# A 512-byte read on each of the sixteen DMA engines, queued ahead of the first load of an RMS norm

## Chip, cores and metric

One core of a Trainium2 chip. The metric is the device time of one execution in microseconds, as the median of several runs. "Span" is the part of an execution that the profile covers; it is about 1.8 us shorter than the measured time. A packet is one piece of a transfer, moved by one of the core's sixteen DMA engines.

## The reference

```python
def setup_inputs():
    batch, seq, dim = 16, 1024, 512
    # x: float32 randn (16, 1024, 512); gamma: ones(512); eps: 1e-5

def reference(x, gamma, eps):
    rms = np.sqrt(np.mean(x ** 2, axis=-1, keepdims=True) + eps)
    x_norm = x / rms * gamma
    return np.maximum(x_norm, 0).astype(np.float32)
```

The input is 33.5 MB and the output as much. The work per element is small, so the transfers decide.

## The kernel before

The rows are cut into eight chunks of 4 MB (16 rows on each of 128 partitions, 32 KB a partition). Six slots in SBUF hold chunks. SyncE, which does no arithmetic here, issues all loads and stores of chunks; the first chunk is loaded in two halves. ScalarE squares and sums, VectorE scales and clamps in place, and the slot is stored from where it lies. GpSimd only turns "load landed" into a count for ScalarE.

```python
    loads = [(0, 0, G), (0, G, K - G)] + [(i, 0, K) for i in range(1, nchunks)]
    ...
    def load(m):
        i, a, r = loads[m]
        nc.sync.dma_start(out=slot_ap(i)[:, a:a + r, :],
                          in_=xv[i][:, a:a + r, :]).then_inc(sem_ld[m], 16)
    ...
    with tc.tile_critical():
        for m, (i, a, r) in enumerate(loads):
            if i < nslots:
                load(m)                      # seven loads, issued at once
        nxt = nslots
        for i in range(nchunks):
            nc.sync.wait_ge(done, per * (i + 1))
            store(i)
            if i >= 1 and nxt < nchunks:
                nc.sync.wait_ge(sem_st[nxt - nslots], 16)
                ...                          # load of chunk nxt into the freed slot
        for m, (i, a, r) in enumerate(loads):
            nc.gpsimd.wait_ge(sem_ld[m], 16)
            nc.gpsimd.sem_inc(ready, r // G)

        nc.vector.memset(gseed, 0.0).then_inc(sem_z, 1)
        nc.vector.memset(eps_sb, eps).then_inc(sem_e, 1)

        nc.scalar.wait_ge(sem_z, 1)
        nc.scalar.dma_start(out=gseed[0:P:32, :], in_=...gamma...).then_inc(sem_g, 16)
        ...                                  # the loops of ScalarE and VectorE
```

## Time and profile before

| | before |
|---|---|
| time, median of six runs | 162.82 us (162.61 to 162.89) |
| span of the profiled run | 161.2 us |
| DMA queue of SyncE, share of sixteen engines | 97.4% |
| VectorE, ScalarE busy | 78%, 54% |
| first load issued, first packet | 0.94 us, 1.95 us |

The prediction was made from three of these runs, whose median was 162.71 us. The transfers are busy from 1.95 us to the end, so a change can only pay off by starting the stream earlier, by losing less of it, or by ending it better. The lines of the profile for this are in the prediction. One line more, for comparison with the kernel after: the instructions of SyncE in order of time, at the start (columns: start, length in us, engine, line, operation, tiles, count).

```profile
0.94 3.59 SPq L74 DMA_DIRECT2D slots<-in_x_dram  x7
```

Seven loads are issued in one go from 0.94 us on, each some 0.4 to 0.7 us of SyncE's time.

### The profile page before, as it was taken

Reading aid. Unit: us, or ns where it says so; the run is one execution under the profiler, and the core shown is the slowest. Engines: PE = TensorE matmul, PEld = TensorE weight load, DVE = VectorE, ACT = ScalarE, POOL = GpSimd, SP = SyncE. Lnnn points to the kernel's source line nnn. Section 1 sums busy time; section 2 is a strip of 40 time slices with the busy share of each in tenths; the row PEclk is TensorE's granted clock in tenths of the full one; section 3 lists DMA queues with packets and bytes.
Section 4 is the critical chain, followed back from the end, with each engine's and each line's share of the span. In section 5 each row is a group of like instructions: output and inputs, shape, how many; then the busy total and the mean of one; then the engine's idle time right before and its main releaser. Section 6 shows DMA issues by size and latency. Waiting matters only on the chain. (4 is left out here: it accounts for less than half of the span.)

```text
span 161.2 us, 1006 instructions
## 1 busy us (share of the span) xinstructions
DVE 126.0 (78%) x164; ACT 86.3 (54%) x273; POOL 0.2 (0%) x4
## 2 busy tenths in 40 slices
DVE  1103989898989898999999999999999999993000
ACT  3088929889988988988900298503994000000000
POOL 0000000000000000000000000000000000000000
DMA  5999999999999999999999999999999999999993
GB/s 155 433 439 431 496 390 415 496 390 399 512 390 390 512 399 390 390 399 512 390 399 504 399 399 496 407 399 488 407 407 488 407 407 480 415 407 464 431 390 138
DMA packets 2456, 67.12 MB, mean 416 GB/s; under 512 B 276, under 2 KB 276, under 8 KB 280
## 3 DMA queue, kind: packets, MB, share of 16 engines
q1 hardware_dynamic: 2448, 67.11, 97.4%
q10 hardware_dynamic: 8, 0.01, 0.0%
HBM read 33.56 MB, written 33.55 MB: 416 GB/s over the span
## 5 line engine op out<-in xcount | busy, mean ns | idle before, releaser
L115 ACT ACTIVATE junk<-slots 128x512 f32 x128 | 74.5, 582 | 30.8 <-ACTq L111 30.5
L139 DVE SCALAR_TENSOR_TENSOR slots<-slots,rstd,gamma_sb 128x512 f32 x128 | 86.2, 747 | 4.8 <-DVEq L136 4.8
L146 DVE TENSOR_SCALAR slots<-slots x16 | 36.7, 2294 | 2.4 <-DVEq L145 0.2
L115 ACT ACTIVATION_READ_ACCUMULATOR junk<-slots x128 | 23.9, 187 | 0.0
L133 DVE RECIPROCAL rstd<-rms x16 | 3.2, 197 | 6.4 <-DVEq L129 6.4
L122 ACT ACTIVATE rms<-ss,eps_sb x16 | 4.8, 301 | 3.0 <-ACTq L121 3.0
L126 DVE LOAD_MASK_SELECT gamma_sb<-gseed x1 | 0.0, 14 | 5.8 <-DMA gseed<-in_gamma_dram 5.8
L107 ACT ACT_TABLE_LOAD x1 | 1.3, 1283 | 2.8 <-issue 2.8
L100 DVE MEMSET gseed<- 128x512 f32 x1 | 0.5, 485 | 1.1 <-SPq L81 1.1
L126 DVE STREAM_SHUFFLE gamma_sb<-gseed 128x512 f32<-128x512 f32 x1 | 0.7, 716 | 0.0
L168 POOL MEMSET const-bfloat16-1.0<- 128x1 bf16 x1 | 0.1, 102 | 0.0
L168 POOL MEMSET const-uint8-127<- 128x1 uint8 x1 | 0.1, 102 | 0.0
L168 POOL MEMSET const-float32-1.0<- 128x1 f32 x1 | 0.1, 99 | 0.0
L168 POOL MEMSET const-float32-0.0<- 128x1 f32 x1 | 0.1, 98 | 0.2 <-issue 0.2
L101 DVE MEMSET eps_sb<- 128x1 f32 x1 | 0.1, 59 | 0.0
## 6 DMA issues: line engine op xcount, KB each, us to landing
out_dram<-slots SPq DMA_DIRECT2D x8, 4096.0 KB, 31.4
slots<-in_x_dram SPq DMA_DIRECT2D x7, 4096.0 KB, 30.4
slots<-in_x_dram SPq DMA_DIRECT2D x2, 2048.0 KB, 9.7
gseed<-in_gamma_dram ACTq DMA_DIRECT2D x1, 8.0 KB
```

The lines of the kernel that those rows point to most:

```text
L100: nc.vector.memset(gseed, 0.0).then_inc(sem_z, 1)
L101: nc.vector.memset(eps_sb, eps).then_inc(sem_e, 1)
L107: nc.scalar.preload_act_table(ACTF.Sqrt)
L115: a = nc.scalar.activation(out=junk[:, j, :], in_=slots[:, bass.ds(base + j * d, d)], func=ACTF.Square, accum_out=ss[:, bass.ds(col + j, 1)])
L122: nc.scalar.activation(out=rms[:, bass.ds(col, G)], in_=ss[:, bass.ds(col, G)], func=ACTF.Sqrt, bias=eps_sb, scale=inv_d).then_inc(sq, 1)
L126: nc.vector.stream_shuffle(gamma_sb, gseed, [0] * 32)
L133: nc.vector.reciprocal(out=rstd[:, bass.ds(col, G)], in_=rms[:, bass.ds(col, G)]).then_inc(sv, 1)
L139: r = nc.vector.scalar_tensor_tensor(out=row, in0=row, scalar=rstd[:, bass.ds(col + j, 1)], in1=gamma_sb, op0=ALU.mult, op1=ALU.mult)
L146: nc.vector.tensor_scalar_max(out=blk, in0=blk, scalar1=0.0).then_inc(done, 1)
L168: nc = _bacc.Bacc("TRN2", target_bir_lowering=False, num_devices=1)
```

## The change

The intent: the first packets of the first load take about twice as long as later ones. A small read on every DMA engine (below: the **touch**), put ahead of that load, might take this start-up loss on itself. Its data is not used.

```diff
+    scratch = singles.tile([16, 128], F32, name="scratch")
...
+    sem_t = tc.alloc_semaphore("touch")
...
     with tc.tile_critical():
+        nc.sync.dma_start(out=scratch, in_=xv[0][0:P:P // 16, 0, 0:128]
+                          ).then_inc(sem_t, 16)
         for m, (i, a, r) in enumerate(loads):
             if i < nslots:
                 load(m)
...
+        nc.gpsimd.wait_ge(sem_t, 16)
         for m, (i, a, r) in enumerate(loads):
             nc.gpsimd.wait_ge(sem_ld[m], 16)
```

## The prediction

> **What bounds the kernel now.** I read the page of the kernel before from its second part down: the engine table, the 40 slices, the DMA queues, then the chain that ended last, the DMA issues, and finally the stretches of time around the start and the end.
>
> ```profile
> span 161.2 us, 1006 instructions
> DVE 126.0 (78%) x164; ACT 86.3 (54%) x273; POOL 0.2 (0%) x4
> DMA  5999999999999999999999999999999999999993
> GB/s 155 433 439 431 496 390 415 496 390 399 512 390 390 512 399 390 390 399 512 390 399 504 399 399 496 407 399 488 407 407 488 407 407 480 415 407 464 431 390 138
> q1 hardware_dynamic: 2448, 67.11, 97.4%
> ```
>
> The reader should see three things. No compute engine is full (VectorE 78%, ScalarE 54%). The DMA row is 9 in every slice but the first and the last, and one queue, SyncE's, keeps the sixteen engines busy for 97.4% of the span. And the two slices that are not full are the ones that the change could touch: the first (5 tenths, 155 GB/s) is the start of the stream. The chain that ended last is of no help here, because it holds only the last VectorE instruction and does not follow the stores.
>
> Is the transfer queue ever short of work? The issues answer it.
>
> ```profile
> core 0 of [0], span 161.2 us
> engine line waited for: us in total, times, longest us
> SPq L78 <- DVE slots L146: 105.4, 6, 26.6
> SPq L74 <- DMA out_dram<-slots: 32.9, 2, 24.1
> SPq L151 <- DMA out_dram<-slots: 12.5, 2, 9.6
> ```
>
> SyncE waits 105.4 us for VectorE before it can issue stores, which looks like a bound by VectorE. It is not: the first store is issued at 31.1 us, but by the trace's completion events the loads already queued land until 62.3 us, so the store stands in the queue behind them. The tightest place is the end: the last store is issued at 146.5 us and the store ahead of it lands at 150.4 us. So VectorE has about 3.9 us in hand where it is tightest, and the stream of transfers alone sets the end. That stream is one line: it starts at some time, then moves 67.1 MB at its rate, and the end is start plus volume over rate. Only the start can move here.
>
> The stretches of time show the start (columns: stretch, its length, VectorE busy, ScalarE busy, GpSimd busy, TensorE clock, DMA share, GB/s; a packet counts where it begins, so short stretches can pass 1.00):
>
> ```profile
> 0.00:0.94 0.94, 0.00 (x0) 0.00 (x0) 0.20 (x4) 1.00 0.00 0
> 0.94:1.90 0.96, 0.49 (x2) 0.00 (x0) 0.00 (x0) 1.00 0.00 0
> 1.90:2.50 0.60, 0.00 (x0) 0.00 (x0) 0.00 (x0) 1.00 1.65 328
> 2.50:3.10 0.60, 0.00 (x0) 0.34 (x1) 0.00 (x0) 1.00 0.29 109
> 3.10:3.70 0.60, 0.00 (x0) 0.60 (x1) 0.00 (x0) 1.00 1.09 437
> 3.70:10.00 6.30, 0.72 (x2) 1.56 (x5) 0.00 (x0) 1.00 0.99 420
> 158.50:161.20 2.70, 0.00 (x0) 0.00 (x0) 0.00 (x0) 1.00 0.00 0
> ```
>
> The first load is issued at 0.94 us and the first packet starts at 1.95 us. In the stretch from 1.90 to 2.50 us, twelve packets of 16 KB begin (328 GB/s times 0.60 us is 197 KB), and their recorded time fills 1.65 of it, far more than such packets normally take; then almost nothing begins until 3.1 us. The packet records say the same one by one: the twelve first packets took 1.18 to 1.49 us (mean 1.32 us), while the later 16 KB packets of the first two loads take 0.611 us. So these engines lose about 0.7 us each on their first packet. The other four engines begin theirs late, at 2.61 to 3.02 us; one of those took 0.92 us, the other three about 0.61. All sixteen first packets end at 3.17 to 3.63 us. If a packet needs 0.611 us of moving, data really moved from 2.56 to 3.02 us at the earliest, whatever start is recorded. This start-up delay is what a small read ahead could be meant to absorb.
>
> **What the Trainium skill says.** "DMA: Bandwidth & Descriptors", section "Where 436 GB/s comes from", gives a ceiling of about 435 GB/s for sixteen engines. This trace agrees: a 32 KB packet takes 1.213 us, so sixteen engines move 16 x 32768 B / 1.213 us = 432 GB/s, and no faster middle is to be had. The same page, section "Latency and other measured facts", gives about 0.6 us to the first byte for a transfer issued from SyncE or ScalarE. The trace shows more: 1.01 us from issue to the first packet's start, and at least 1.6 us to the first data moving. The section "Queues, rings and completion order" says that on each engine descriptors are consumed in ring order and a later one may finish its write earlier. So the sixteen touches go ahead of the load's own descriptors, and the load is not held for their writes. The section "Why a DMA increments its semaphore by 16 and not by 1" says how many engines a copy uses: the largest number up to 16 that divides both outer dimensions. Both are 16 here, so each engine gets one 512-byte read, as intended. The trace of the kernel before cannot show these last two; the order and the number of packets after can. No section I found says that a first read warms anything.
>
> **The change, part by part.**
>
> It removes nothing. It adds one SyncE issue ahead of the first load, sixteen 512-byte packets with sixteen semaphore writes, one wait on GpSimd, and an unused tile of 512 bytes on 16 partitions.
>
> 1. The issue. The first two loads are issued at 0.94 and 1.375 us, 0.435 us apart, so the first load should now be issued near 1.375 us and its first packet can start at 1.95 + 0.435 = 2.38 us. All later issues move back alike, but they queue behind a full stream and cost nothing.
>
> 2. The packets. In the trace, a 2048-byte packet of the gamma load takes 84 ns and a 4-byte semaphore write 9 ns. In a straight line between them, 512 bytes take an estimated 28 ns; with its semaphore write, 37 ns on each engine. All of it lies on the stream: +0.04 us.
>
> 3. The start-up delay. It now falls on the touch, which is issued when the load was (0.94 us), so it ends when it ended before, at 2.56 to 3.02 us. The load's descriptors, there from 2.38 us on, wait behind it and then run at 0.611 us. That hides the issue delay of step 1 but wins nothing, because the delay runs from the same time: the touch can start no earlier than the load did. For the twelve early engines the net is step 2's +0.04 us. The four engines that started last (2.61, 2.83, 2.84, 3.02 us) may start their load 0.435 us later again if their lateness comes from the handing out of descriptors and not from the first access. Then the net there is up to +0.43 us.
>
> 4. GpSimd's wait for the touch ends by about 3.5 us, well before the first load lands at 8.4 us, where its next wait ends. Free. If ScalarE starts 0.2 us later than its 8.78 us, VectorE's path moves back by the same, against 3.9 us in hand. Free too.
>
> Sum: between +0.04 and +0.43 us; I take the middle, +0.2 us, so 162.71 + 0.2 = 162.9 us.
>
> **The rivals.**
>
> The warm-up wins. If what makes first packets slow is the load's large form (its 128 descriptors) and a small touch gets past it quicker, first packets would run at 0.611 us from 2.38 us on and end at about 3.0 us in place of a mean of 3.4 us: -0.4 us, or 162.3 us. For it: the mean excess of 0.7 us exceeds the 0.435 us that the touch costs. Against it: all sixteen first packets end within 0.46 us, even those that began a microsecond later, which looks like a delay from the start of traffic and not like a cost of each packet.
>
> The warm-up fails. If the excess belongs to the load's own first write into its tile, or to its own source pages on the remaining partitions, it is paid after the touch again. Then the whole issue delay stays: +0.435 + 0.04 = +0.47 us, or 163.2 us; should the touch's own delay be added in full, some +0.7 us more, 163.9 us. For it: the touch writes to another tile than the load. Against it: of the sixteen second packets most take 0.611 us at once, though they too are first accesses to their rows.
>
> VectorE takes over the end. It would need a shift of over 3.9 us between the first landing and the stores; nothing in a touch of under a microsecond makes that. In that case the time would be above 166 us.
>
> The phases change. One late engine ends the last store at 160.04 us, 0.83 us after the fifteenth (159.21 us), and near 58 to 60 us twenty-two packets of 32 KB stretch from 1.21 to as much as 1.96 us. If such events depend on the engines' phase, a shift at the start may add or take several tenths at random. This widens the range to both sides.
>
> **Range and chances.** The middle is +0.2 us. The runs before spread by 0.28 us, the two rivals of the warm-up stand at -0.4 and +0.5 us, and the phases add perhaps 0.3 us. I take 162.5 to 163.4 us for 8 in 10. Two per cent is 3.25 us: more than the entire loss at the start and four times the last engine's lag. Faster by that much I give 0.01, slower 0.01.
>
> **What would show it.** Step 1: the first load's issue near 1.38 us, the touch's at 0.94. Step 2: sixteen packets of 512 bytes, each followed by no gap. Step 3: the touch packets, or the gap behind them, carry the start-up delay, the first 16 KB packets take close to 0.611 us, and those end at 3.2 to 3.9 us. The warm-up wins if they end by 3.1 us; it fails if they still take 1.2 us and end at 3.7 us or later. Throughout, the DMA row stays at 9 and the rate from 10 to 60 us at 434 GB/s. I am wrong in the main if the time moves by over 0.7 us, for then something other than the start of the stream has changed, such as the pace of the slowest engine.

## The result, and the profile after

The changed kernel takes 163.36 us (163.20 to 163.51, six runs) against 162.82 us before. The ratio is 1.0034, with a 95% interval of 1.0022 to 1.0047: a true loss of about half a microsecond. Ratios in this text are the mean time of one kernel's runs over the mean of the other's of the same rounds, so they are not quite the ratio of the medians quoted.

The page of the changed kernel, the lines that answer to those shown of before:

```profile
span 161.6 us, 1007 instructions
DMA  4999999999999999999999999999999999999993
GB/s 116 416 434 466 406 479 414 406 487 406 406 487 406 406 422 414 446 389 454 454 398 446 454 389 454 454 389 454 446 398 454 446 398 454 446 397 454 446 397 130
q1 hardware_dynamic: 2480, 67.12, 97.1%
...
scratch<-in_x_dram SPq DMA_DIRECT2D x1, 8.0 KB, 1.7
```

Only the first slice has changed in kind: 4 tenths and 116 GB/s in place of 5 and 155. The queue holds 32 packets more (2480 against 2448): sixteen reads and sixteen semaphore writes. SyncE's instructions at the start show the shift:

```profile
0.94 0.39 SPq L85 DMA_DIRECT2D scratch<-in_x_dram  x1
1.39 3.64 SPq L76 DMA_DIRECT2D slots<-in_x_dram  x7
```

The touch takes the place at 0.94 us, and the first load comes 0.45 us later. The stretches of time at the start (columns as in the prediction: stretch, length, VectorE, ScalarE, GpSimd, TensorE clock, DMA share, GB/s by packets begun):

```profile
1.90:2.50 0.60, 0.00 (x0) 0.00 (x0) 0.00 (x0) 1.00 0.55 123
2.50:3.10 0.60, 0.00 (x0) 0.35 (x1) 0.00 (x0) 1.00 1.06 218
3.10:3.70 0.60, 0.00 (x0) 0.60 (x1) 0.00 (x0) 1.00 0.55 164
3.70:10.00 6.30, 0.72 (x2) 0.85 (x2) 0.00 (x0) 1.00 0.99 423
```

Before, 328 GB/s of packets began in the first of these stretches and full rate was there by the third (437). Now the slow start is spread over 2.4 to 3.7 us, and full rate comes only after. The packet records give the detail. The sixteen touches start between 1.95 and 2.34 us and take 25 ns each, with 9 ns for the semaphore: they run into no delay at all. The load's first sixteen packets start between 2.41 and 3.31 us and take 1.15 us on average (0.75 to 1.67), against 1.16 us before and 0.611 us in full flow. They end at a mean of 3.91 us, before at 3.41 us.

To follow such a shift through a run I use one number, the **lag of the stream**: at some time, that time minus the bytes moved so far at 432 GB/s (32 KB in 1.213 us on sixteen engines). Packets that are under way count in proportion. While the engines are full it stays constant. At 13 us it is 2.90 us before and 3.40 us after. The difference, 0.50 us, is there from 5 us on (2.87 and 3.37) and still there at 57 us (2.84 and 3.35). So the loss comes out of the first 5 us.

### The profile page after: what moved, and what is told of

It is laid out like the page before. It is cut to its first block, busy times and chain, and to the rows that moved or that the text cites. A ratio compares the mean times of both kernels' runs of the same rounds, so it can differ in the third digit from the quotient of the medians.

```text
span 161.6 us, 1007 instructions
## 1 busy us (share of the span) xinstructions
DVE 126.0 (78%) x164; ACT 86.3 (53%) x273; POOL 0.2 (0%) x4
## 3 DMA queue, kind: packets, MB, share of 16 engines
q1 hardware_dynamic: 2480, 67.12, 97.1%
```

## The experiments

The theory after the result: the touch warms nothing, and costs the 0.45 us of SyncE's time by which it pushes the first load back (**the issue slot**). Rivals: the touch's packets or their semaphore disturb the stream; or the touch does help but its gain is eaten. And one question beside it: what is the slow start? A first form of two of the kernels, with timed NOPs on SyncE, could not be simulated and never ran (the record holds nothing of it); the delays below wait for a VectorE memset instead.

| kernel | time us | before beside it | ratio (95%) | first load issued | first 16 KB packets, mean us | lag at 13 us |
|---|---|---|---|---|---|---|
| before | 162.82 | | | 0.94 | 1.16 | 2.90 |
| the change | 163.36 | 162.82 | 1.0034 (1.0022 to 1.0047) | 1.39 | 1.15 | 3.40 |
| e1_touch_on_act | 162.86 | 162.88 | 1.0003 (0.9991 to 1.0015) | 0.94 | 1.27 | 2.93 |
| e2_touch_second | 162.84 | 162.88 | 1.0001 (0.9988 to 1.0013) | 0.94 | 1.23 | 2.83 |
| e3_delay_only | 163.19 | 162.88 | 1.0016 (1.0003 to 1.0029) | 1.10 | 1.26 | 3.02 |
| e4_touch_16kb | 163.82 | 162.88 | 1.0051 (1.0039 to 1.0064) | 1.38 | 0.85 | 2.78 |
| e5_hold_second | 162.94 | 162.98 | 1.0006 (0.9992 to 1.0019) | 0.94 | 1.19 | 2.83 |
| e6_restart | 165.36 | 162.98 | 1.0152 (1.0137 to 1.0167) | 0.94 | 1.12 | 5.17 |
| e7_gamma_late | 163.03 | 162.98 | 1.0005 (0.9990 to 1.0019) | 0.94 | 1.18 | 2.91 |
| e8_touch_landed | 164.68 | 162.98 | 1.0107 (1.0089 to 1.0125) | 2.61 | 1.18 | 4.46 |
| e9_delay_045 | 163.47 | 162.92 | 1.0028 (1.0003 to 1.0053) | 1.45 | 1.06 | 3.37 |
| after_again | 163.32 | 162.92 | 1.0017 (0.9994 to 1.0041) | 1.39 | 1.26 | 3.35 |
| e11_two_touches | 164.09 | 162.92 | 1.0066 (1.0041 to 1.0091) | 1.85 | 1.27 | 4.00 |
| e10_first_row | 162.98 | 162.92 | 0.9994 (0.9971 to 1.0018) | 0.94 | 0.79 (14 KB) | 2.89 |

The last three columns come from the trace of one profiled run of each. A 14 KB packet takes 0.538 us in flow, so the 0.79 us of e10 is 0.25 us over. Kernels with the same neighbour were run together on one chip.

### The touch issued from ScalarE

```diff
-        nc.sync.dma_start(out=scratch, ...).then_inc(sem_t, 16)
+        nc.scalar.dma_start(out=scratch, ...).then_inc(sem_t, 16)
```

> The touch is issued from ScalarE, beside SyncE's first load, so it takes no issue slot ahead of the load. Theory of the issue slot (the touch warms nothing and costs only SyncE's 0.45 us): the load is issued near 0.94 us again and the time is that of the kernel before, 162.8 us (within 0.15). Rival (the touch's own packets or its semaphore disturb the stream): it stays at 163.2 us or more. Rival (the touch does warm, but its gain was eaten by the slot): 162.1 to 162.5 us, first 16 KB packets close to 0.611 us.

Measured: 162.86 us, ratio 1.0003. The order of time in its trace:

```profile
0.91 0.43 ACTq L85 DMA_DIRECT2D scratch<-in_x_dram  x1
0.94 3.82 SPq L76 DMA_DIRECT2D slots<-in_x_dram  x7
```

The load is back at 0.94 us and the loss is gone, though the same sixteen packets run. The kernel does not test the warm-up: the touch was issued at 0.91 us, but its packets started only at 2.90 us, when the load's were already under way. An issue from ScalarE was no quick way ahead.

### The touch behind the first load

```diff
+        load(0)
         nc.sync.dma_start(out=scratch, ...).then_inc(sem_t, 16)
         for m, (i, a, r) in enumerate(loads):
-            if i < nslots:
+            if 0 < m and i < nslots:
```

> The touch is issued after the first load and before the second, on the same queue. Issue slot: the first load starts as in the kernel before, the queue has 4.9 us of work when the later loads come 0.45 us later, so the time is 162.8 us plus at most 0.04 us for the packets. Rival (the packets or the extra wait cost the half microsecond, wherever they stand): 163.2 to 163.4 us.

Measured: 162.84 us, ratio 1.0001. SyncE's issues at the start:

```profile
0.94 0.39 SPq L76 DMA_DIRECT2D slots<-in_x_dram  x1
1.38 0.42 SPq L86 DMA_DIRECT2D scratch<-in_x_dram  x1
1.85 3.23 SPq L76 DMA_DIRECT2D slots<-in_x_dram  x6
```

Same issue, same packets, same wait on GpSimd, same queue, but one place later: no loss that the interval (-0.2 to +0.2 us) can show. What costs is to stand ahead of the first load.

### A delay without a touch, first try

```diff
     with tc.tile_critical():
+        nc.sync.wait_ge(sem_e, 1)
...
-        nc.vector.memset(gseed, 0.0).then_inc(sem_z, 1)
         nc.vector.memset(eps_sb, eps).then_inc(sem_e, 1)
+        nc.vector.memset(gseed, 0.0).then_inc(sem_z, 1)
```

> No touch at all; SyncE waits for a small VectorE memset that is moved to the front, which should put the first load's issue at 1.3 to 1.4 us in place of 0.94. Issue slot: the loss comes back without any touch: time before plus that shift, 163.2 to 163.3 us, and first packets as slow as after the touch (mean 1.1 to 1.3 us). Rival (the touch makes the load's first packets slower, or quicker): a time off that by over 0.2 us and different first packets.

Measured: 163.19 us. The delay missed its size: the load was issued at 1.10 us, 0.16 us late and not 0.45, since the memset that it waits for, now VectorE's first, began at 1.01 us and took 0.06 us. The lag rose by 0.12 us. The time rose by 0.05 to 0.47 us (the interval times 162.88 us), which holds 0.16 us but settles little.

### The same delay in its right size

```diff
     with tc.tile_critical():
+        nc.sync.wait_ge(sem_p, 1)
...
+        nc.vector.memset(pad, 0.0).then_inc(sem_p, 1)     # pad: [128, 336] f32
         nc.vector.memset(gseed, 0.0).then_inc(sem_z, 1)
```

> No touch; SyncE waits for a VectorE memset of 128x336 elements put ahead of all others, which ends near 1.33 us, so that the first load is issued near 1.38 us as in the change (the earlier delay kernel reached only 1.10 us). Issue slot alone: the loss of the change in full, a ratio of 1.002 to 1.004 over the kernel before, and not apart from the change run again beside it. If the touch costs beyond its slot (its packets, its state): 0.2 us or more below the change. If the touch also helps: above it.

> The changed kernel again, on the chip of the other three kernels of this call, so that they can be compared within one set of rounds: 163.3 to 163.5 us, 0.3 to 0.6 us above the kernel before.

Measured: 163.47 us for the delay, 163.32 us for the change beside it. The first load of the delay kernel:

```profile
1.45 3.44 SPq L76 DMA_DIRECT2D slots<-in_x_dram  x7
```

It was issued 0.51 us later than before, and its lag is 0.47 us higher; for the change the two are 0.45 and 0.45 us in this run (0.50 in the first). So a pure delay makes the loss in full, with no touch in the program. The runs of the kernel before scattered more than usual (162.71 to 163.80), so the intervals are wide: the ratio of the change run again does not even exclude 1. The traces, not these intervals, carry this reading.

### Two touches

```diff
         nc.sync.dma_start(out=scratch, ...).then_inc(sem_t, 16)
+        nc.sync.dma_start(out=scratch2, ...).then_inc(sem_t, 16)
...                                          # GpSimd waits for 32 in place of 16
```

> Two touches ahead of the first load, so two issue slots. Issue slot: twice the loss of the change, 0.45 us above it, near 163.8 us, the first load's issue near 1.83 us. If the loss is something met once (any small read ahead): 163.4 us as with one.

Measured: 164.09 us, 0.77 us above the change beside it, where 0.45 was expected. The loss is not met once; it grows with each touch. It grew by more than a slot: the load was issued at 1.85 us, 0.46 us later than with one touch, but the lag rose by 0.65 us (3.35 to 4.00), since the load's first packet came 1.27 us after its issue and not some 1.03. Why a second small transfer in the queue adds 0.2 us beyond its slot stays open. The profiled run, at 163.80 us, was the quickest of its six, so its lag cannot be set against the median of 164.09 us to the last tenth.

### The load held until the touch has landed

```diff
         nc.sync.dma_start(out=scratch, ...).then_inc(sem_t, 16)
+        nc.sync.wait_ge(sem_t, 16)
```

> The touch as in the change, but SyncE waits until it has landed (2.65 us) before it issues the first load, which then comes near 2.8 us, 1.85 us later than before. If a finished first read leaves a warm state (the load came too soon behind it to profit): first packets about 0.61 to 0.7 us, time 162.8 + 1.85 - 0.6 = 164.1 us. If the touch warms nothing: first packets 1.2 us or more, time 164.6 us.

Measured: 164.68 us, and first packets of 1.18 us. The stretches at the start of the load:

```profile
3.50:4.10 0.60, 0.56 (x2) 0.54 (x1) 0.00 (x0) 1.00 1.79 382
4.10:4.70 0.60, 0.16 (x1) 0.00 (x0) 0.00 (x0) 1.00 0.17 55
4.70:5.30 0.60, 0.00 (x0) 0.00 (x0) 0.00 (x0) 1.00 1.11 437
```

A first read on every engine, landed by 2.59 us, 1.0 us before the load's first packet (3.58 us), leaves no state that helps: 164.1 was expected of a warm state, 164.6 of none. Nor did it help in the change itself, where the load's first packets start from 2.41 us on and the last touch has ended at 2.36. Rests between these two were not tested.

### A pause after the first load

```diff
                 load(m)
+                if m == 0:
+                    nc.sync.wait_ge(sem_ld[0], 16)
```

> The kernel before, but SyncE waits for the first load to land (8.4 us) before it issues the second, so that the engines go quiet for over a microsecond and start again. If the slow first packets are a cold state met once: the packets after the pause take 0.611 us each from the first. If every start from rest of sixteen engines is slow: they take 1.2 us or more again. The time rises by the pause, 1.5 us (0.6 more if the start is slow again): 164.3 to 165.0 us.

Measured: 165.36 us, somewhat more than either theory gave. The stretches around the start and around the restart:

```profile
1.90:2.50 0.60, 0.00 (x0) 0.00 (x0) 0.00 (x0) 1.00 1.63 355
2.50:3.10 0.60, 0.00 (x0) 0.35 (x1) 0.00 (x0) 1.00 0.24 82
3.10:3.70 0.60, 0.00 (x0) 0.60 (x1) 0.00 (x0) 1.00 1.05 437
8.40:9.10 0.70, 0.00 (x0) 0.51 (x1) 0.00 (x0) 1.00 0.00 0
9.10:9.70 0.60, 0.00 (x0) 0.60 (x3) 0.00 (x0) 1.00 1.95 410
9.70:10.30 0.60, 0.00 (x0) 0.60 (x3) 0.00 (x0) 1.00 0.09 27
10.30:10.90 0.60, 0.00 (x0) 0.60 (x3) 0.00 (x0) 1.00 1.08 437
```

The two groups of three look alike: many packets begin at once, then almost none for 0.6 us, then full rate. After the pause, at 9.17 us and with 2 MB moved, the first sixteen 16 KB packets again take 1.22 us on average, and the next sixteen 0.65. So the slow start is no cold state that is met once: it came at both starts of sixteen engines from rest, and a read ahead of the stream starts from rest too. The lag rose by 2.36 us, from 2.81 to 5.17: by 1.32 us while the engines stood empty (7.85 to 9.17 us), by some 0.17 us while the first load ran out, and by 0.87 us in the second slow start, which cost as much as the first (1.95 us at the first packet, lag 2.80 at 5 us: 0.85 us).

### Two suspects for the slow start

Hold the other loads back, so that nothing is made ready while the first load's packets start:

```diff
                 load(m)
+                if m == 0:
+                    nc.sync.wait_ge(sem_p, 1)     # a long memset of VectorE
```

> The kernel before, but SyncE issues only the first load at 0.94 us and waits for a long VectorE memset (to about 3.7 us) before the other loads; the first load alone keeps the engines busy to 7.9 us. If the slow first packets come from the following loads being made ready at the same time (descriptors written while data moves): first packets drop to about 0.6 to 0.7 us and the time falls by up to 0.6 us, to 162.2 us. If the start of traffic itself is slow: first packets still 1.2 to 1.5 us, time 162.8 us (within 0.15).

Measured: 162.94 us, first packets 1.19 us. The second load was issued at 3.78 us, after the slow phase. It is not the making of the following loads; the making of the first load's own packets was not tested.

Hold ScalarE's gamma load back:

```diff
         nc.scalar.wait_ge(sem_z, 1)
+        nc.scalar.wait_ge(sem_ld[0], 16)
```

> The kernel before, but ScalarE's small gamma load, issued at 1.63 us and 1.09 us long, waits until the first load has landed. If that issue from a second engine disturbs the making of the first load's descriptors: first packets drop, the four late engines start near 2.3 us, and the time falls by 0.3 us or more. If not: 162.8 us (within 0.15) and first packets as before.

Measured: 163.03 us, first packets 1.18 us, and the lag at 13 us is 2.91 as before. It is not the other engine's issue either. The time alone would not show that, for this kernel has a loss of its own at the end: ScalarE begins 2.0 us later, the last store is issued 2.0 us later (148.54 us), and the lag rises from 3.58 at 148 us to 3.92 at 150 us. Eleven engines stood empty for 0.2 to 0.75 us until that store's first packets came at 149.38 us. These packets then took 1.22 us each against 1.213 in flow: no slow start. But they are stores, five engines were still busy, and the rest was short; which of these matters was not tested.

### A touch of 16 KB for each engine

```diff
-    scratch = singles.tile([16, 128], F32, name="scratch")
+    scratch = singles.tile([P, 512], F32, name="scratch")
-        nc.sync.dma_start(out=scratch, in_=xv[0][0:P:P // 16, 0, 0:128] ...
+        nc.sync.dma_start(out=scratch, in_=xv[0][:, 0, :] ...
```

> The touch is 2 KB on each of 128 partitions, 16 KB for each engine, ahead of the first load. If the start-up loss is paid once by the first packets of some size (a cold start that 512 bytes are too little to use up): the touch takes it, the load's first packets run near 0.611 us; the time is that of after plus about 0.67 us for the bytes, minus what of the 0.7 us is no longer paid twice: it is paid once either way, so 163.9 to 164.1 us. If it belongs to each load's own rows or to a 16 KB packet form: it is paid in the load again, first 16 KB packets 1.2 us or more, time 164.2 us or more.

Measured: 163.82 us. Here the load's first packets take only 0.85 us. Its stretches:

```profile
1.90:2.50 0.60, 0.00 (x0) 0.00 (x0) 0.00 (x0) 1.00 0.69 143
2.50:3.10 0.60, 0.00 (x0) 0.34 (x1) 0.00 (x0) 1.00 1.72 556
3.10:3.70 0.60, 0.00 (x0) 0.60 (x1) 0.00 (x0) 1.00 0.61 201
```

The empty stretch in the middle is gone; the 2 KB packets flow through it, 105 of 128 at 81 to 99 ns and the others, mostly among the first, at up to 562 ns. Counted with the touch's own 262 KB, the lag at 13 us is 2.78 us, 0.12 under that of before. Without them it is 2.78 + 0.61 = 3.39 us (262 KB at 432 GB/s take 0.61 us), the same as for the 512-byte touch.

My expectation was worked out wrongly: it added the slot and the bytes, but the bytes move while the slot passes. Paid once means the lag of before plus the bytes, 2.90 + 0.61 = 3.51 us; paid again in full means some 0.6 us more. The measured 3.39 us speaks for once, with a part paid again (0.85 us against 0.611 for a first packet) and a milder start on the small packets. So a touch that is large enough takes about half of the first packets' excess on itself (0.24 us is left of 0.55), but then its bytes cost what it saves, and the useful data come no sooner than with the small one. This touch reads rows that the load reads again; e10 below, where it does not, leaves the same 0.25 us. The time is higher than this lag says: the trace of this run loses another half microsecond between 30 and 50 us (lag 2.76 to 3.31), which no other trace shows and which I cannot explain. All five runs lie above those of the change (163.55 to 163.87 us against 163.20 to 163.51), but only one has a trace.

### Useful small packets first

The last result suggests making the first packets small but useful: the first row (2 KB) of each partition as its own load, then the other seven.

```diff
-    loads = [(0, 0, G), (0, G, K - G)] + ...
+    loads = [(0, 0, 1), (0, 1, G - 1), (0, G, K - G)] + ...
...                                          # GpSimd's count adjusted to the cut
```

> No touch; the first load is cut into its first row of 2 KB on each partition and the other seven, so that the stream starts with small packets that are needed anyway. The 16 KB touch suggested a milder start with 2 KB packets (data counted in full it was 0.1 us ahead of the kernel before). If small first packets escape a part of the start-up loss: 162.7 us, up to 0.2 us under the kernel before. If not, or if the extra issue and packets cost as much: 162.8 to 163.0 us, the same.

Measured: 162.98 us against 162.92, ratio 0.9994 (0.9971 to 1.0018). At 5 us the lag was 2.79 in place of 2.87 us, but by 13 us it was 2.89 against 2.90. No gain that these runs can show, and no version beats the kernel before.

## Why the prediction was right or wrong

The time, 163.36 us, lies in the range (162.5 to 163.4), 0.04 us from its upper edge, and "within 2%" was right. That it lies inside owes much to the width: the range was drawn to hold the rival "The warm-up fails" (163.2 us) and a margin for the engines' phases. The centre, 162.9 us, was too low by 0.46 us. Of this, 0.11 us is the start, the median of three runs (162.71) in place of six (162.82); the rest comes from one step.

- **What bounds the kernel**: right. The stream keeps its rate (434 GB/s from 10 to 60 us in both traces) and the end moves with the start.
- **Step 1, the issue**: right in itself. The first load is issued at 1.39 us where 1.375 was predicted, its first packet starts at 2.41 where 2.38 was predicted, and e9 shows that such a delay alone makes the loss.
- **Step 2, the packets**: right and small. A touch packet took 25 ns and its semaphore 9 ns, together 34 where 37 was estimated. e1 and e2, which have the packets without the slot, cost nothing measurable. The touches start before every packet of the load (1.95 to 2.34 us, then 2.41), and there are sixteen of them, as the prediction expected.
- **Step 3, the start-up delay**: wrong. The step said "It now falls on the touch". The touches ran at once, 25 ns each, and the load's first packets paid the whole slow start after them (1.15 us against 1.16). The evidence taken for a delay that runs from the start of traffic was that all first packets ended within 0.46 us of one another, from which the prediction worked out that data moved "from 2.56 to 3.02 us at the earliest". That does not follow: a packet that needs 0.611 us and ends at 3.17 us has begun to move by 2.56 at the latest, and may have moved slowly since 1.95. e4 shows that data do move earlier: its first 2 KB packet had ended at 2.06 us and 35 of the 128 by 2.56 us. What fits the runs is a slow rate under the first large packets, not a dead time on the first access; whether the bytes or the size of the packets count is not shown. With step 3 gone, nothing hides step 1, and the term "+0.04 to +0.43" becomes 0.435 + 0.04 = 0.47 us. That is what the rival "The warm-up fails" gave (163.2 us); its cause, the load's own tile or pages, does not fit the runs: after the pause in e6 the first packets are slow although they go on in the same tile and read the rows next to those just loaded, and the sixteen after them, as new to their rows, take 0.65 us. The prediction's own sign for this rival (1.2 us, ends at 3.7 us or later) is what came.
- **Step 4, GpSimd and VectorE**: right in effect, wrong in size. The first load landed at 9.09 in place of 8.38 us, so ScalarE began 0.70 us later and not 0.2. VectorE's last result came 0.70 us later too, and the last store was issued at 147.22 us. That cost nothing, but the room was far smaller than the 3.9 us that the prediction measured to the landing of the store ahead (150.78 us now). The store's packets must be there when the first engine has finished the store ahead, which was at 148.66 us before and 149.06 with the change (the first semaphore write), and in e7 they came 0.84 us after the issue. So I estimate the room at 148.66 - 146.52 - 0.84 = 1.3 us before and 149.06 - 147.22 - 0.84 = 1.0 us with the change. e7 bears this out: 2.0 us of delay left engines empty for up to 0.75 us there and cost 0.34 us of lag, although the store ahead landed 1.9 us after the issue.
- **The rivals**: the warm-up did not win, in any placement. VectorE did not take over, though 2.0 us would have been enough to begin it (e7), not 3.9.

Shown: the cost of the change is the first load's delay by one issue. Not shown: why large packets start slowly from rest. It is not the preparation of later loads (e5), not gamma's issue (e7), not a state that one small read sets up and that lasts 1.0 us (e8), and not a thing of the program's first moments (e6).

## What to carry to other kernels

In a kernel that is bound by its transfers, the first useful transfer should be the first thing its queue issues: what was put ahead of it here, only 8 KB in all, cost a full issue (0.45 us), while the same thing one place later cost nothing measurable. Before you pay for a warm-up, ask whether the loss is tied to the first access or comes with every start from rest; a pause in the middle of the program (e6) tells in one run. Read the duration of the warm-up's own packets: where all of them run at one normal speed, as here (25 ns), nothing shows that they have met the loss or taken any of it. And when you ask how long an engine may be late, count to the moment at which the queue begins to run dry, not to the landing of the transfer ahead (here an estimated 1.3 us against 3.9).

## What the Trainium skill lacked or had wrong

- "DMA: Bandwidth & Descriptors", section "Latency and other measured facts", gives about 0.6 us to the first byte for SyncE and ScalarE and does not say from where it counts. From the start of SyncE's issue to the first packet it was 1.0 us here (0.94 to 1.95 us), which the prediction took for a difference; from the end of the issue (0.94 + 0.39 = 1.33 us) it was 0.62 us, and 0.62 us again in e8 (2.96 to 3.58), which agrees with the page. On ScalarE, with a load of SyncE issued beside it, it was 1.56 us from the end of the issue (1.34 to 2.90 us in e1), which the page does not have.
- No page that I read has the slow start from rest: the first 16 KB packets of sixteen engines took 1.16 us on average against 0.611 us in flow, and again 1.22 us after a pause in mid-program (e6). The table in "DMA: Bandwidth & Descriptors", section "Measured (HBM→SBUF, 128 partitions, SWDGE, issued from GpSimd)", gives efficiency by size of one transfer alone, and does not say that a first transfer in a stream pays this.
- No page that I read says that the lag of a full stream jumps where the first stores come in: between 57 and 65 us the stream of the kernel before lost 0.7 us (lag 2.84 to 3.55), and every other run lost 0.5 to 0.9 us there. No experiment here looked for its cause.
- No page that I read says how far the slowest of the sixteen engines falls behind: the last store's slowest engine ended 0.83 us after the fifteenth before, 0.65 us after it with the change, and 0.1 us in e2. This scatter is as large as the effect under study, which is why the lag is the better measure.
